# First block's attention: both key groups in one pass over the softmax, their matmuls on alternate halves of the array, compression in four column groups

## Chip, cores and metric

The kernel runs on one core of one Trainium2 chip. The metric is the device time of one execution in microseconds (us); the median of the runs shown is what is to be predicted.

## The reference

Two blocks of two layers each work on 256 tokens of width 1024, all in float32. Only the attention of the first block is touched by the change. Its branch A is compressed, selected and windowed attention, branch B a sliding window with sinks, branch C a latent attention:

```python
def nsa_attention(q, kc, vc, ks, vs, kw, vw, gate_logits, ...):
    G, R, dh = A_KV_GROUPS, A_HEADS // A_KV_GROUPS, HEAD_DIM      # 2, 4, 64
    k_cmp = compress_blocks(kc, tok, pos_k, w1_k, w2_k)           # gelu(flat @ w1) @ w2
    v_cmp = compress_blocks(vc, tok, pos_v, w1_v, w2_v)
    ...
    s = jnp.einsum('bqgrd,bngd->bgrqn', qc, k_cmp) * scale        # compressed
    ...
    s = jnp.einsum('bqgrd,bgqkd->bgrqk', qc, kb) * scale          # selected
    o_sel = jnp.einsum('bgrqk,bgqkd->bqgrd', p_sel, vb)
    s = jnp.einsum('bqgrd,bkgd->bgrqk', qc, kwc) * scale          # window
    o_win = jnp.einsum('bgrqk,bkgd->bqgrd', p_win, vwc)
    return gc[..., 0:1] * o_cmp + gc[..., 1:2] * o_sel + gc[..., 2:3] * o_win

merged = g_a * (o_a @ w_branch_a) + g_b * (o_b @ w_branch_b) + g_c * (o_c @ w_branch_c)
```

Branches A and B have 8 heads in 2 groups; the 4 heads of a group share keys and values of width 64.

## The kernel before

Linear layers split weights and activations into two float32r parts, `hi` and `lo` (`chunk` and `split`, lines 287 to 301): a chunk of 128x1024 weights is loaded by SP's queue into one of three `raw` buffers, ScalarE casts `hi` (L289) and VectorE subtracts `lo` (L290). Three matmuls (`mm3`, L305 to L307) replace one. A linear layer is a generator that yields after each chunk (12 matmuls of 512 columns where rows are tokens), so that it can be taken in steps. `first_layer` puts the gates of the branches and their output projections into the list `todo`, and `fill(n)` (L349) emits n chunks of it. Where a step stands in the program is then only a wish: a scheduler that knows the dependencies moves the instructions of each engine, and the order that results is fixed before the run.

`attention` (L638) has the stages B, C, compress (L809) and A, in this order. In B and A, a loop over two query tiles t of 128 tokens and over the two groups g calls `soft` for one group: for t = 0 one PSUM bank holds 4 heads of 128 keys, for t = 1 two banks hold 2 heads of 256 keys each. A bank starts with a mask (L537, bf16, an identity as weights) to which the scores are added (L685 in `heads`: the contraction is over the 64 rows of group g, rows 0 to 63 or 64 to 127). Then come the maximum (L542), the exponentials (L548), `fill(2)`, the reciprocal and the scaling (L557 to L562), the transposes into `ptp` (L567) and the copies to `PT` (L570, L572). `pv_group` (L575) multiplies with the values: 64 output columns, PSUM partitions 64g to 64g+63 of the bank `pob` or `poa`. A does this twice (kinds 0 and 1). C (L753, L759) works on four heads of one kind at a time; its value matmuls go to alternate halves of `poc`'s partitions for t = 0.

`compress` makes for keys and then for values a sum over 16 steps (L836): each has 32 weight columns (`kp`) and 256 columns of a raw float32 chunk, 4 steps to a chunk, all into partitions 0 to 31 of one bank. A GELU (L839), a transpose (L844) and a small matmul follow. The compressed scores are L777.

PSUM's 8 banks are shared out by `open_psum(3, 2, 3)`: 3 for linear layers, 2 for `po`, 3 short-lived ones.

A matmul of two float32 operands stands in the trace as two records, called passes here; a transpose, a bf16 or a float32r matmul as one.

## Time and profile before

| what | value |
|---|---|
| median of 3 runs | 3464.09 us (3457.46 to 3465.89) |
| the profiled execution | 3465.89 us, span 3465.9 us |
| TensorE (PE) busy | 3340.5 us, 96% of the span |
| VectorE (DVE), ScalarE (ACT) busy | 65%, 51% |
| mean granted TensorE clock | 0.985 of 2.4 GHz |

The profile shows one execution. Times of rows count from the start of the span. A matmul's duration reaches from its start to a modelled end, and the next starts before that end; how fast a row of matmuls runs is therefore read from start to start. Layer 0's attention lies at about 82 to 288 us, layer 1's at about 638 to 847 us.

### The profile page before, as it was taken

What the parts mean: (1) busy time and instruction counts of PE and PEld (TensorE: products, weight loads), DVE (VectorE), ACT (ScalarE), POOL (GpSimd) and SP (SyncE); (2) the same over time, 40 slices, a digit from 0 to 9 for tenths busy, and PEclk for the clock granted to TensorE, in tenths of its full rate; (3) what the DMA queues carried; (4) which work ended last, traced back from release to release, by engine and by line L of the source; (5) the groups of instructions that cost most, each with busy time, mean ns of one, the idle gap of its engine ahead of it and who ended that gap; (6) DMA issues with size and microseconds to landing.
All of it is one profiled execution on the core that took longest, in us unless ns stands there. A gap on an engine that the chain in (4) does not pass through costs nothing.

```text
span 3465.9 us, 53945 instructions
## 1 busy us (share of the span) xinstructions
PE 3340.5 (96%) x20862; PEld 2926.5 (84%) x20862; DVE 2255.5 (65%) x3879; ACT 1760.3 (51%) x3218; POOL 238.8 (7%) x159
## 2 busy tenths in 40 slices
PE   8999999999999999998999999998989899999999
PEld 6767998766898887898988999988879898899998
DVE  6646556646556875669965555557657996555555
ACT  4535445534445554444964444447444395444444
POOL 0000000000000000037000000000003700000000
PEclk9999999999999999998999999999999999999999
DMA  5344666443555444553255555555544415555555
GB/s 185 106 128 161 213 201 203 137 128 109 188 186 183 152 149 136 188 177 128 68 168 188 187 187 189 189 182 190 168 161 152 140 56 182 188 187 185 188 188 177
DMA packets 161105, 570.00 MB, mean 164 GB/s; under 512 B 18256, under 2 KB 23760, under 8 KB 159824
## 3 DMA queue, kind: packets, MB, share of 16 engines
q1 hardware_dynamic: 160848, 566.56, 49.7%
q8 instruction: 163, 2.67, 0.3%
q14 instruction: 94, 0.77, 0.1%
HBM read 557.05 MB, written 9.44 MB: 163 GB/s over the span
## 4 chain that ended last, share of the span: by engine, by line
PE 61%; DVE 10%; DMA 2%; ACT 2%; issue 1%; POOL 0%; DVEq 0%; POOLq 0%; ACTq 0%; SPq 0%
PE pacc L305 7%; PE pacc L307 7%; PE pacc L306 7%; PE aps L305 4%; PE aps L306 4%; PE aps L307 4%; PE ps L305 3%; PE ps L307 3%; PE ps L306 3%; PE gps L1681 3%; PE ps L1674 2%; PE fps L306 1%; PE fps L305 1%; PE fps L307 1%; DVE G L1767 1%; DVE lo L290 1%
## 5 line engine op out<-in xcount | busy, mean ns | idle before, releaser
L290 DVE TENSOR_TENSOR lo<-raw,hi 128x1024 fp32r<-128x1024 f32 (+3 forms) x906 | 1103.1, 1218 | 791.5 <-ACT hi L289 788.0
L289 ACT CAST hi<-raw 128x1024 fp32r<-128x1024 f32 (+1 forms) x978 | 1019.4, 1044 | 953.3 <-PE aps L306 182.4
L305 PE MATMUL pacc<-hi,pwh 128*128 128x512 f32 x1024 | 404.4, 395 | 0.1
L307 PE MATMUL pacc<-hi,pwl 128*128 128x512 f32 x1024 | 403.7, 394 | 0.0
L306 PE MATMUL pacc<-lo,pwh 128*128 128x512 f32 x1024 | 402.9, 393 | 0.0
L305 PE MATMUL aps<-xTh,hi 128*128 128x256 f32 x1296 | 365.1, 282 | 0.9 <-ACT G L1684 0.9
L306 PE MATMUL aps<-xTl,hi 128*128 128x256 f32 x1296 | 365.0, 282 | 0.0
L307 PE MATMUL aps<-xTh,lo 128*128 128x256 f32 x1296 | 363.6, 281 | 0.0
L305 PE MATMUL ps<-xTh,hi 128*128 128x256 f32 x960 | 278.4, 291 | 16.3 <-ACT hi L289 12.5
L307 PE MATMUL ps<-xTh,lo 128*128 128x256 f32 x960 | 277.8, 289 | 15.8 <-POOL lo L290 15.8
L289 ACT CAST pwh<-G 128x256 fp32r<-128x256 f32 x256 | 103.8, 406 | 342.7 <-DVE G L1689 213.9
L306 PE MATMUL ps<-xTl,hi 128*128 128x256 f32 x960 | 276.6, 288 | 1.2 <-DVE xTl L290 1.2
L305 PEld LDWEIGHTS aps<-xTh,hi 128*128 128x128 f32 x1296 | 243.8, 188 | 7.8 <-ACT G L1684 1.3
L306 PEld LDWEIGHTS aps<-xTl,hi 128*128 128x128 f32 x1296 | 243.7, 188 | 7.2
L307 PEld LDWEIGHTS aps<-xTh,lo 128*128 128x128 f32 x1296 | 243.8, 188 | 0.0
L307 PEld LDWEIGHTS pacc<-hi,pwl 128*128 128x128 f32 x1024 | 192.4, 188 | 45.9 <-DVE pwl L290 0.3
L305 PEld LDWEIGHTS pacc<-hi,pwh 128*128 128x128 f32 x1024 | 192.6, 188 | 39.0 <-ACT pwh L289 1.0
L306 PEld LDWEIGHTS pacc<-lo,pwh 128*128 128x128 f32 x1024 | 193.1, 189 | 37.9
L290 POOL TENSOR_TENSOR lo<-raw,hi 128x1024 fp32r<-128x1024 f32 x72 | 192.8, 2688 | 178.5 <-ACT hi L289 177.6
L305 PE MATMUL fps<-fTh,hi 128*128 128x256 f32 x704 | 199.6, 284 | 3.7 <-ACT fTh L289 3.6
L305 PEld LDWEIGHTS ps<-xTh,hi 128*128 128x128 f32 x960 | 187.6, 196 | 18.1 <-ACT hi L289 13.3
L307 PEld LDWEIGHTS ps<-xTh,lo 128*128 128x128 f32 x960 | 187.2, 195 | 17.5 <-POOL lo L290 17.2
(649 smaller groups left out, 7043.4 us busy)
## 6 DMA issues: line engine op xcount, KB each, us to landing
raw<-in_pu_dram SPq DMA_DIRECT2D x256, 512.0 KB, 3.3
raw<-in_pv_dram SPq DMA_DIRECT2D x256, 512.0 KB, 3.3
raw<-in_wbg_dram SPq DMA_DIRECT2D x48, 512.0 KB, 3.5
raw<-in_ffg_dram SPq DMA_DIRECT2D x44, 512.0 KB, 3.6
raw<-in_ffu_dram SPq DMA_DIRECT2D x44, 512.0 KB, 3.4
raw<-in_ffd_dram SPq DMA_DIRECT2D x44, 512.0 KB, 3.8
raw<-in_win_dram SPq DMA_DIRECT2D x36, 512.0 KB, 3.5
raw<-in_pwq_dram SPq DMA_DIRECT2D x32, 512.0 KB, 3.9
```

Source lines behind the costliest of these rows:

```text
L289: self.nc.scalar.copy(out=hi, in_=src)
L290: (eng or self.nc.vector).tensor_tensor(out=lo, in0=src, in1=hi.bitcast(F32), op=OP.subtract)
L305: mm(ps, lhsT=lh, rhs=rh, start=start, stop=False)
L306: mm(ps, lhsT=lh, rhs=rl, start=False, stop=False)
L307: mm(ps, lhsT=ll, rhs=rh, start=False, stop=stop)
L1674: nc.tensor.matmul(pi, lhsT=w[:, k * P:k * P + P], rhs=xT32[:, k], start=k == 0, stop=k == 7)
L1681: nc.tensor.matmul(ps[:, t * P:t * P + P], lhsT=A[:, t], rhs=B[:, t], start=True, stop=True)
L1767: nc.vector.tensor_tensor(out=cv[:, h], in0=vv[:, h, 0, :, None].to_broadcast([P, 16, 16]), in1=vv[:, h, 1, None, :].to_broadcast([P, 16, ...
```

## The change

- `soft` takes a list of score functions. For both groups it issues the two masks, then the scores head by head, group 0 and group 1 in turn; maxima, exponentials and sinks of both follow, then one `fill(4)`, then scaling, transposes and copies of group 0 and of group 1.
- `pv_groups` issues the value matmuls of both groups in turn for each key tile. In C the value matmuls go in turn to the two halves for t = 1 too.
- The compressed scores go in turn to two banks, one a group.
- In `compress` step j of a chunk goes to the PSUM partitions 32j to 32j+31. The four sums are copied to SBUF (`hq`, ScalarE) and added by a matmul with a 128x32 selection matrix `sel` into a new bank (`chs`).
- PSUM is shared out as 3, 1, 4.

```diff
-    def soft(self, pool, t, score_mm, mask, weight, sink=None):
+    def soft(self, pool, t, scores, mask, weights, sinks=None):
...
         for u in range(nk):
-            ps = self.bank("sc")
-            nc.tensor.matmul(ps.rearrange("p (a b) -> p a b", a=mask.shape[1]), lhsT=self.identb, rhs=mask, start=True, stop=False)
+            pss = [self.bank("sc") for _ in range(n)]
+            for ps in pss:
+                nc.tensor.matmul(ps.rearrange("p (a b) -> p a b", a=mask.shape[1]), lhsT=self.identb, rhs=mask, start=True, stop=False)
             for j in range(hb):
-                score_mm(ps[:, j * nk * P:(j + 1) * nk * P], u * hb + j, j == hb - 1)
...
+                for ps, score_mm in zip(pss, scores):
+                    score_mm(ps[:, j * nk * P:(j + 1) * nk * P], u * hb + j, j == hb - 1)
...
-        self.fill(2)
+        self.fill(2 * n)
...
-    def pv_group(self, ps, t, g, PT, v, start, stop):
+    def pv_groups(self, ps, t, PTs, v, start, stop):
...
         for kt in range(t + 1):
-            self.nc.tensor.matmul(ps[g * 64:g * 64 + 64, :], lhsT=v(kt), rhs=PT[:, kt].rearrange("p h q -> p (h q)"),
-                                  start=start and kt == 0, stop=stop and kt == t)
+            for g in range(2):
+                self.nc.tensor.matmul(ps[g * 64:g * 64 + 64, :], lhsT=v(kt, g), rhs=PTs[g][:, kt].rearrange("p h q -> p (h q)"),
+                                      start=start and kt == 0, stop=stop and kt == t)
...
-            self.open_psum(3, 2, 3)
+            self.open_psum(3, 1, 4)
...
-                    nc.tensor.matmul(hp[0:32, 0:256], lhsT=kp[:, jj].rearrange("p g n -> p (g n)"),
-                                     rhs=w[:, j * 256:j * 256 + 256], start=jj == 0, stop=jj == 15)
+                    nc.tensor.matmul(hp[j * 32:j * 32 + 32, 0:256], lhsT=kp[:, jj].rearrange("p g n -> p (g n)"),
+                                     rhs=w[:, j * 256:j * 256 + 256], start=c4 == 0, stop=c4 == 3, tile_position=(0, j * 32))
+
+            hq = ap.tile([P, 256], F32, tag="chq", name="chq", bufs=1)
+            nc.scalar.copy(out=hq, in_=hp[:, 0:256])
+            hs = self.bank("chs")
+            nc.tensor.matmul(hs[0:32, 0:256], lhsT=sel, rhs=hq, start=True, stop=True)
             hid = ap.tile([32, 256], F32, tag="chid", name="chid", bufs=2)
-            nc.scalar.activation(out=hid, in_=hp[0:32, 0:256], func=AF.Gelu_apprx_tanh)
+            nc.scalar.activation(out=hid, in_=hs[0:32, 0:256], func=AF.Gelu_apprx_tanh)
```

The order of SP's loads and of GpSimd's instructions is the same before and after, and so is TensorE's outside the two attentions but for a few rows. Three places on TensorE follow. In a row stand line, operation, output and inputs with buffer numbers, and the output's size; xN is a run of N.

Stage B of layer 0, between the first query tile and the second (`sc` scores, `mb` mask, `ptp` transposes, `pob` values, `ps` linear layer). Before:

```order
L567 MATMUL ptp_905<-cst_142,Pt_843 128x128 x4
L537 LDWEIGHTS identb_149
L537 MATMUL sc_918<-mb_156,identb_149 128x512
L685 MATMUL sc_918<-kT_247,qTb_246 128x256 x2
L578 MATMUL pob_772<-PT_904,vt_248 64x512
L537 LDWEIGHTS identb_149
L537 MATMUL sc_926<-mb_156,identb_149 128x512
L685 MATMUL sc_926<-kT_247,qTb_246 128x256 x2
L305 MATMUL ps_938<-hi_942,hTh_178 128x512
```

Now:

```order
L574 MATMUL ptp_904<-cst_142,Pt_774 128x128 x4
L539 LDWEIGHTS identb_149
L539 MATMUL sc_921<-mb_156,identb_149 128x512
L539 LDWEIGHTS identb_149
L539 MATMUL sc_922<-mb_156,identb_149 128x512
L588 MATMUL pob_772<-PT_892,vt_248 64x512
L588 MATMUL pob_772<-PT_903,vt_248 64x512
L695 MATMUL sc_921<-kT_247,qTb_246 128x256
L695 MATMUL sc_922<-kT_247,qTb_246 128x256
L695 MATMUL sc_921<-kT_247,qTb_246 128x256
L695 MATMUL sc_922<-kT_247,qTb_246 128x256
```

Scores of one group stood in a row and now alternate between the groups (`sc_921`, `sc_922`); the two value matmuls stand side by side.

Stage B of layer 0, after the second query tile's transposes. Before:

```order
L567 MATMUL ptp_981<-cst_142,Pt_915 128x128 x4
L567 MATMUL ptp_987<-cst_142,Pt_915 128x128 x4
L537 LDWEIGHTS identb_149
L537 MATMUL sc_998<-mb_156,identb_149 128x512
L685 MATMUL sc_998<-kT_247,qTb_246 128x256 x2
L578 MATMUL pob_914<-PT_980,vt_248 64x512 x2
```

Now:

```order
L574 MATMUL ptp_1059<-cst_142,Pt_916 128x128 x4
L574 MATMUL ptp_1065<-cst_142,Pt_916 128x128 x4
L588 MATMUL pob_914<-PT_1041,vt_248 64x512
L588 MATMUL pob_914<-PT_1058,vt_248 64x512
L588 MATMUL pob_914<-PT_1041,vt_248 64x512
L588 MATMUL pob_914<-PT_1058,vt_248 64x512
L389 MATMUL trp_1091<-cst_142,cxn_1083 128x128 x2
```

Mask and scores of the other group stood between transposes and values; now the values follow the transposes at once.

From compress to A in layer 0 (`chp` compression, `chs` the added sum, `scm` compressed scores). Before:

```order
L836 MATMUL chp<-raw,kp 32x256 x16
L844 MATMUL chT<-cst,chid 128x32 x2
L853 MATMUL cko<-chTk,cw2d 128x32 x2
L821 MATMUL cps<-cst,vt 64x64 x8
L836 MATMUL chp<-raw,kp 32x256 x16
L305 MATMUL ps<-hi,oTh 128x512 x2
L844 MATMUL chT<-cst,chid 128x32 x2
L306 MATMUL ps<-lo,oTh 128x512
```

Now:

```order
L847 MATMUL chp<-raw,kp 32x256 x16
L853 MATMUL chs<-chq,csel 32x256
L860 MATMUL chT<-cst,chid 128x32 x2
L869 MATMUL cko<-chTk,cw2d 128x32 x2
L832 MATMUL cps<-cst,vt 64x64 x8
L847 MATMUL chp<-raw,kp 32x256 x16
L853 MATMUL chs<-chq,csel 32x256
L860 MATMUL chT<-cst,chid 128x32 x2
```

Each half has one matmul more, and no row of a linear layer stands in the stage any longer.

## Rows read from the trace of the kernel before

**Rows 1.** The page: busy time and its share of the span, by engine.

```profile
PE 3340.5 (96%) x20862; PEld 2926.5 (84%) x20862; DVE 2255.5 (65%) x3879; ACT 1760.3 (51%) x3218; POOL 238.8 (7%) x159
```

**Rows 2.** By stretch: us, busy PE, PEld, DVE, ACT, POOL, granted clock, DMA share, GB/s.

```profile
82.10:124.50 42.40, 41.87 (x181) 28.39 (x181) 26.22 (x50) 22.72 (x61) 0.00 (x0) 1.00 0.37 119
...
175.50:200.30 24.80, 20.80 (x111) 11.19 (x111) 5.14 (x16) 4.75 (x6) 0.53 (x1) 0.92 0.58 188
200.30:288.00 87.70, 87.70 (x374) 58.79 (x375) 54.77 (x91) 38.42 (x95) 0.31 (x1) 0.98 0.34 108
...
757.00:847.50 90.50, 90.50 (x375) 61.04 (x375) 54.84 (x91) 38.35 (x95) 0.31 (x1) 0.95 0.33 104
```

**Rows 3.** Timeline of PE in stage B: start, us, engine, line, what, count.

```profile
90.58 0.38 PE L537 MATMUL sc<-mb,identb 128*128 128x512 bf16 x1
90.89 1.16 PE L685 MATMUL sc<-kT,qTb 64*128 64x128 f32 x8
91.98 0.50 PE L306 MATMUL ps<-lo,hTh 128*128 128x512 f32 x1
92.40 1.07 PE L578 MATMUL pob<-PT,vt 128*64 128x512 f32 x2
93.41 0.50 PE L307 MATMUL ps<-hi,hTl 128*128 128x512 f32 x1
93.75 0.39 PE L305 MATMUL ps<-hi,hTh 128*128 128x512 f32 x1
93.98 0.39 PE L306 MATMUL ps<-lo,hTh 128*128 128x512 f32 x1
```

**Rows 4.** Tiles sc, pob, poa, scm: passes of the run, ns min/median/max, forms.

```profile
L685 PE MATMUL sc<-kT,qTa x128: 272/376/579, 203.7 to 833.4; 64*128 64x128 f32 x64, 64*128 64x256 f32 x64
...
L578 PE MATMUL pob<-PT,vt x24: 592/592/644, 92.4 to 678.8; 128*64 128x512 f32 x24
...
L578 PE MATMUL poa<-PT,vt x48: 592/592/643, 213.4 to 845.7; 128*64 128x512 f32 x48
...
L777 PE MATMUL scm<-kcT,qTa x64: 259/259/373, 198.7 to 798.2; 64*128 64x16 f32 x64
```

**Rows 5.** Timeline of PE in stage A: runs on one half alone.

```profile
235.21 1.06 PE L777 MATMUL scm<-kcT,qTa 64*128 64x16 f32 x8
...
249.51 1.93 PE L578 MATMUL poa<-PT,vt 128*64 128x512 f32 x4
```

**Rows 6.** Timeline of PE: runs where two halves meet (C, compress, second block).

```profile
139.74 0.66 PE L759 MATMUL poc<-PT,vc 128*64 128x128 f32 x8
...
198.90 0.84 PE L777 MATMUL scm<-kcT,qTa 64*128 64x16 f32 x10
...
2441.80 0.83 PE L1552 MATMUL hsp<-hv,hf 64*128 64x128 f32 x9
```

**Rows 7.** Timeline of all engines in compress, layer 0.

```profile
175.56 7.09 PE L836 MATMUL chp<-raw,kp 128*32 128x256 f32 x32 [0.61 <-PE cps L821]
177.47 0.33 SPq L295 DMA_DIRECT2D raw<-in_cw1k_dram  x1
...
185.83 8.75 PE L836 MATMUL chp<-raw,kp 128*32 128x256 f32 x32 [0.85 <-DVE kp L829]
...
196.59 0.72 PE L305 MATMUL ps<-hi,oTh 128*128 128x512 f32 x2 [2.01 <-ACT hi L289]
```

**Rows 8.** Tile raw, 172 to 200 us: load issue to landing.

```profile
DMA to landing us min/median/max: 3.2/4.1/4.7
```

**Rows 9.** Groups of DVE, 80 to 300 us: busy, mean ns, idle before.

```profile
L290 DVE TENSOR_TENSOR lo<-raw,hi 128x1024 fp32r<-128x1024 f32 x40 | 48.9, 1221 | 22.0 <-ACT hi L289 21.8
L572 DVE COPY PT<-ptp 128x512 f32<-128x512 f32 x16 | 11.0, 690 | 11.7 <-PE ptp L567 11.7
L542 DVE TENSOR_REDUCE nm<-sc 128x2 f32<-128x512 f32 x16 | 10.9, 688 | 10.1 <-PE sc L685 9.0 <-PE sc L753 1.1
L562 DVE TENSOR_TENSOR Pt<-Pt,rc 128x1024 f32<-128x1024 f32 x8 | 9.8, 1225 | 0.3
```

More of the change, by code (lines that the diff above doesn't have):

```diff
@@ L531, in soft @@
         hb = 4 // nk
-        Pt = pool.tile([P, 4, 2 * P], F32, tag="Pt", name="Pt", bufs=2)[:, :, :nk * P]
-        nm = pool.tile([P, 4], F32, tag="nm", name="nm", bufs=4)
-        sm = pool.tile([P, 4], F32, tag="sm", name="sm", bufs=4)
+        n = len(scores)
+        Pts = [pool.tile([P, 4, 2 * P], F32, tag="Pt", name="Pt", bufs=2)[:, :, :nk * P] for _ in range(n)]
+        nms = [pool.tile([P, 4], F32, tag="nm", name="nm", bufs=4) for _ in range(n)]
+        sms = [pool.tile([P, 4], F32, tag="sm", name="sm", bufs=4) for _ in range(n)]
@@ L550, in soft @@
-        if sink is not None:
-            es = pool.tile([P, 4], F32, tag="es", name="es", bufs=2)
-            nc.vector.tensor_tensor(out=es, in0=sink, in1=nm, op=OP.add)
-            nc.scalar.activation(out=es, in_=es, func=AF.Exp)
-            nc.vector.tensor_tensor(out=sm, in0=sm, in1=es, op=OP.add)
-        self.fill(2)
-        rc = pool.tile([P, 4], F32, tag="rc", name="rc", bufs=4)
-        nc.vector.reciprocal(rc, sm)
-        if weight is not None:
-            nc.vector.tensor_tensor(out=rc, in0=rc, in1=weight, op=OP.mult)
-        else:
-            nc.vector.tensor_scalar(rc, rc, 0.5, None, op0=OP.mult)
@@ L562, in soft @@
-        nc.vector.tensor_tensor(out=Pt, in0=Pt, in1=rc[:, :, None].to_broadcast([P, 4, nk * P]), op=OP.mult)
-        PT = pool.tile([P, 2, 4, P], F32, tag="PT", name="PT", bufs=2)
-        for kt in range(nk):
-            ps = self.bank("ptp")
-            for h in range(4):
-                nc.tensor.transpose(ps[:, h * P:h * P + P], Pt[:, h, kt * P:kt * P + P], self.ident)
-            dst = PT[:, kt].rearrange("p h q -> p (h q)")
-            if kt:
-                nc.scalar.copy(out=dst, in_=ps)
-            else:
-                nc.vector.tensor_copy(dst, ps)
@@ L573, in soft @@
-        return PT
-    def pv_group(self, ps, t, g, PT, v, start, stop):
+                for ps, score_mm in zip(pss, scores):
+                    score_mm(ps[:, j * nk * P:(j + 1) * nk * P], u * hb + j, j == hb - 1)
+            for i in range(n):
+                pv = pss[i].rearrange("p (j k) -> p j k", j=hb)
+                hs = slice(u * hb, u * hb + hb)
+                nc.vector.tensor_reduce(out=nms[i][:, hs], in_=pv, axis=AX, op=OP.max, negate=True)
+                if sinks is not None:
+                    nc.vector.scalar_tensor_tensor(out=nms[i][:, hs], in0=sinks[i][:, hs], scalar=-1.0, in1=nms[i][:, hs],
+                                                   op0=OP.mult, op1=OP.min)
+                for j in range(hb):
+                    h = u * hb + j
+                    nc.scalar.activation(out=Pts[i][:, h], in_=pv[:, j], func=AF.Exp, bias=nms[i][:, h:h + 1],
+                                         accum_out=sms[i][:, h:h + 1])
@@ new lines, in soft @@
+        if sinks is not None:
+            for sink, nm, sm in zip(sinks, nms, sms):
+                es = pool.tile([P, 4], F32, tag="es", name="es", bufs=2)
+                nc.vector.tensor_tensor(out=es, in0=sink, in1=nm, op=OP.add)
+                nc.scalar.activation(out=es, in_=es, func=AF.Exp)
+                nc.vector.tensor_tensor(out=sm, in0=sm, in1=es, op=OP.add)
+        self.fill(2 * n)
+        PTs = []
+        for i in range(n):
+            rc = pool.tile([P, 4], F32, tag="rc", name="rc", bufs=4)
+            nc.vector.reciprocal(rc, sms[i])
+            if weights is not None:
+                nc.vector.tensor_tensor(out=rc, in0=rc, in1=weights[i], op=OP.mult)
+            else:
+                nc.vector.tensor_scalar(rc, rc, 0.5, None, op0=OP.mult)
+            nc.vector.tensor_tensor(out=Pts[i], in0=Pts[i], in1=rc[:, :, None].to_broadcast([P, 4, nk * P]), op=OP.mult)
+            PT = pool.tile([P, 2, 4, P], F32, tag="PT", name="PT", bufs=2)
+            for kt in range(nk):
+                ps = self.bank("ptp")
+                for h in range(4):
+                    nc.tensor.transpose(ps[:, h * P:h * P + P], Pts[i][:, h, kt * P:kt * P + P], self.ident)
+                dst = PT[:, kt].rearrange("p h q -> p (h q)")
+                if kt:
+                    nc.scalar.copy(out=dst, in_=ps)
+                else:
+                    nc.vector.tensor_copy(dst, ps)
+            PTs.append(PT)
@@ L813, in compress @@
         nc.gpsimd.memset(V2, 0.0)
+        sel = ap.tile([P, 32], F32, name="csel")
+        nc.vector.tensor_reduce(out=sel, in_=self.ident.rearrange("p (j n) -> p n j", j=4), axis=AX, op=OP.add)
         for s in "kv":
```

44 lines of the change are left out of this document (17 added, 27 removed).

## The prediction

> **What bounds the kernel now.** I read the page first: TensorE is busy for 96% of the span, VectorE for 65%, ScalarE for 51% [rows 1]. An average hides stages, so the table by stretch came next. In stage B of layer 0 TensorE is busy for 41.87 of 42.40 us, in stage A for all of 87.70; VectorE has 26.22 and 54.77 us there [rows 2]. The reader is to see that `fill` covers the softmax fully: time taken off TensorE in B and A comes off the run, as long as VectorE does not become the next bound. Compress is different: busy for 20.80 of 24.80 us at a mean granted clock of 0.92, with little else to do [rows 2]. Last came the timeline, read from start to start, for what a pass and a change of the array's shape cost.
>
> **Prices.** A lone 64-row pass of 128 columns or fewer takes (1.06 - 0.26) / 7 = 0.114 us [rows 4, 5]. A pass of 256 columns takes (7.09 - 0.38) / 31 = 0.216 us in compress's run of 32 [rows 7]; 0.38 is how long one such pass lasts, the median of the `sc` row, whose longer half are the 256-column passes [rows 4]. A value pass of 512 columns takes (1.93 - 0.59) / 3 = 0.45 us with the run's slow first one, 0.43 without [rows 4, 5]. A linear matmul starts every 0.23 us (93.75 to 93.98) [rows 3].
>
> Now the change of shape. From 90.58 to 93.75 stand a mask, 8 score passes, a linear matmul, 2 value passes and another linear one: 3.17 us [rows 3]. At the prices above they need 0.23 + 8 x 0.113 + 0.23 + 2 x 0.43 + 0.23 = 2.45. The other 0.72 us fall to four changes between whole array, row halves and column halves: **0.18 us each**.
>
> **Do two halves overlap?** This kernel already has places where they meet. In C eight passes of 128 columns on alternate column halves last 0.66 us [rows 6]; the last starts 0.66 - 0.27 = 0.39 after the first [a pass of 128 columns lasts 0.27 at least, rows 4], where one half alone would need 7 x 0.114 = 0.80. For row halves, ten passes of the compressed scores where the groups meet start every (0.84 - 0.26) / 9 = 0.064 us, nine of the second block's 64-row passes every (0.83 - 0.27) / 8 = 0.07, against 0.114 alone [rows 5, 6]. So both kinds run side by side in float32, and I take the longer of two equal runs: half.
>
> **The sum for one layer.** A has 32 score passes of 128 and 32 of 256 columns a layer (rows 4, two layers), B half as many; the scores stand alternately now.
> - Scores: of 48 passes of 128 columns 24 go, 24 x 0.113 = 2.7 us; of 48 of 256 columns 24 go, 24 x 0.216 = 5.2. Together 7.9.
> - Values: 72 passes in both layers [rows 4], 36 in one; 18 x 0.43 = 7.7.
> - Compressed scores: 64 passes in both [rows 4], 32 in one; 16 x 0.114 = 1.8.
> - Changes of shape outside compress, counted in the two whole orders for one layer: 75 before, 44 now. 31 x 0.18 = 5.6.
> - C's values alternate already at t = 0; the second tile gains a few tenths, taken as nothing. Masks, transposes, exponentials, copies, fill chunks and loads keep their number. A's first pair changes shape once more between its two masks; that is in the 44.
> - Bound from the other side: new waits. In four of a layer's six pairs the values follow the transposes at once, where a mask and scores stood between. They then wait for a copy of 0.69 us [rows 9]: 4 x 0.7 = 2.8 lost. One `po` bank in place of two costs nothing: four fill chunks (4 x 12 x 0.23 = 11 us) stand between the last read of one and the first write of the next.
>
> **Compress.** The keys' 32 passes took 7.09 us, and the fourth chunk's load, which waits for the first chunk's buffer, went out at 177.47, 1.91 after the start [rows 7]. In four column groups a chunk of 8 passes needs 2 x 0.216 = 0.43, so this load goes out 1.3 earlier, about 176.2, lands 3.2 later [rows 8] at 179.4, and the keys end near 179.8 in place of 182.65. From there to the values' start it was 185.83 - 182.65 = 3.2 us; the added copy, the matmul of two passes and their handovers make it about 4.4 (0.4 + 0.6 + 0.2, an estimate from the 256-column pass and a shape change). The values start at 184.2; their fourth load goes out 0.5 later, lands 4.1 later at 188.8, and they end at 189.2, where it was 185.83 + 8.75 = 194.58. The second added chain gives back 1.2: **4.2 us gained**, bound by loads instead of matmuls. Ends: all the matmul time saved, three quarters of 64 x 0.216, 10.4; or nothing, with both chains paid, -2.4. No row shows four column groups at once, but two at once would move the end by less than 1 us, since the loads decide.
>
> Sum: 7.9 + 7.7 + 1.8 + 5.6 + 4.2 - 2.8 = 24.4 a layer, 48.8 for two. The profiled execution took 3465.9, 1.8 above the median; 3465.9 - 48.8 = 3417.1, and against the median **3415**.
>
> **Rivals.**
> *VectorE takes over (0.15).* B's 26.22 us of VectorE now stand in about 35 us, A's 54.77 in about 72: 75%. A second-tile pair has four maxima (2.8 us), small steps (about 1.8), two scalings (2.4) and up to four `lo` (4.9) in one queue, 11.9 us, and some 2 us of exponentials inside the chain, against 11.1 us of fill [rows 9]. If all of it comes before the last transposes, 2.9 us a pair are open, some 0.7 for a first-tile pair: 3 x 3.6 = 10.8 a layer, leaving 13.6, 27 in all: 3437. Against: in ScalarE's order three chunks' `hi` stand ahead of A's first exponentials, and in VectorE's only one `lo` between B's two scalings. The Trainium skill, "TensorEngine Tiling (Array Packing)", section "PSUM Bottleneck", states this rule: packing speeds up TensorE but not the emptying of PSUM, which may become the bound. No row here shows it happening yet.
>
> *A slot lost in each run (0.07).* Every float32 matmul is two passes of one half. If starts keep program order strictly, the first group's second pass must go before the second group's first, and each run takes one slot more: three runs of 0.113, six of 0.216 and six of 0.43 a layer, 4.2 us, leaving 40: 3424. Against: four matmuls on alternate halves would need five slots, a last start at 4 x 0.114 = 0.46; it was 0.39 [rows 6]. The Trainium skill, "TensorE: Matmul & The Clock Gate", section "Part 3: Packing small matmuls — row/col tiling", says just this of order, and also that a weight load passes running matmuls only where the row group differs. By that, column pairs would also wait for each load of 64 columns, by its price for a load, columns over 1.2 GHz, 53 ns each: an estimate of 36 x 0.053 = 1.9 us a layer more, 3428 with the lost slots. The trace's 0.66 us for eight passes on column halves disagrees.
>
> *It does not do what it says (0.08).* The long passes do not overlap, say because two streams of 256 or 512 columns cannot be read at once; the rows that overlap have 16 to 128. Only the shapes and compress remain: 5.6 + 4.2 - 2.8 = 7.0, 14 in all: 3450.
>
> *Slower, by the clock (0.03).* In compress TensorE stood at its lower level of 1.2 GHz for 2 x 0.08 x 24.8 = 4 us, and in the A after it for 3.5 us in layer 0 and 9 in layer 1 [rows 2]. Now compress has a quarter of its matmul time and longer idle stretches. If the clock then stayed low through both A stages (2 x 72 us, less the 12.5 they lose part of already), the run takes 143 - 6 = 137 us more for that and 49 less for the change: 3552. It decides where 98 us more are spent at the lower level. Against: in B, with many small passes, the clock was 1.00, and the longest stretch at the lower level is those 9 us [rows 2].
>
> **How the numbers follow.** The forecast has 0.67, with its own range 3397 (no new waits, 10.4 in compress) to 3428 (compress at -2.4). With the first two rivals that makes 0.89, so the range is 3397 to 3440. About 0.3% (10 us) is what a measurement of this kernel can tell from no change: forecast, both first rivals and half of the third are faster, 0.93; the other half the same, 0.04; slower 0.03.
>
> **What would show it.** Right: `sc` and value passes of both groups start in twos, some 10 ns apart, at the lone pass's pace; B shorter by some 6 us, A by 15; TensorE still busy throughout in both; the loads' landing, not matmuls, ending the waits in compress. Wrong: `ptp` waiting for `Pt` (VectorE), `pob` and `poa` for `PT` by more than 0.7 each, a granted clock in A under 0.9, or single starts at 0.216 and 0.43.

## The result

The changed kernel takes 3419.33 us (median of four runs, 3416.98 to 3424.47), the kernel before 3464.80 beside it. The ratio is **0.9874**, 95% interval 0.9861 to 0.9887. The prediction was 3415 (3397 to 3440). The profiled execution of the changed kernel has a span of 3419.2 us; all that follows is read from it and from the profiled executions of the experiments.

The page, busy time by engine, beside [rows 1]:

```profile
PE 3283.9 (96%) x20870; PEld 2901.5 (85%) x20870; DVE 2251.0 (66%) x3881; ACT 1759.0 (51%) x3222; POOL 240.1 (7%) x159
```

TensorE lost 56.6 us of busy time and the span 46.7, with the share at 96% as before. Nearly all of the difference is compress's, where TensorE lost 17.3 busy us and the stage only 7.9 (next two tables).

By stretch, first the kernel before, cut at marks that every run has: stage B of layer 0 (first mask to last `pob` pass), compress (first `cps` to first `scm` pass) and stage A (first `scm` to last value pass) of layer 0, then the last two of layer 1. Every mark is the start of its pass. The columns are those of [rows 2].

```profile
82.12:122.20 40.08, 39.95 (x174) 27.33 (x174) 25.08 (x47) 21.04 (x55) 0.00 (x0) 1.00 0.36 116
172.94:198.65 25.71, 21.16 (x128) 11.41 (x127) 5.04 (x16) 4.90 (x7) 0.53 (x1) 0.93 0.50 164
198.65:287.15 88.50, 88.50 (x389) 60.14 (x388) 55.74 (x95) 39.24 (x95) 0.31 (x1) 0.98 0.34 109
729.50:755.28 25.78, 21.16 (x129) 11.50 (x128) 4.75 (x16) 5.26 (x8) 0.53 (x1) 0.93 0.50 163
755.28:846.72 91.44, 91.44 (x389) 62.50 (x388) 56.22 (x95) 38.97 (x95) 0.31 (x1) 0.94 0.33 105
```

The same five stretches of the changed kernel:

```profile
80.70:114.11 33.41, 33.41 (x170) 24.39 (x170) 23.04 (x46) 20.23 (x54) 0.00 (x0) 1.00 0.46 139
165.11:186.01 20.90, 12.22 (x130) 6.99 (x129) 3.19 (x14) 4.78 (x8) 0.53 (x1) 0.78 0.55 194
186.01:263.31 77.30, 77.02 (x387) 55.92 (x387) 56.76 (x96) 39.84 (x96) 0.31 (x1) 0.95 0.39 126
698.03:720.71 22.68, 12.78 (x129) 7.08 (x128) 3.19 (x14) 5.14 (x9) 0.53 (x1) 0.75 0.56 186
720.71:798.55 77.84, 77.56 (x388) 56.30 (x387) 56.76 (x96) 39.18 (x96) 0.31 (x1) 0.94 0.39 123
```

B of layer 0 is 6.7 us shorter (part of it, 0.9 us, are four transposes that now stand behind B), A 11.2 and 13.6, compress 4.8 and 3.1. In B and A TensorE is still busy throughout. In compress it is not: 12.22 of 20.90 us, where it had 21.16 of 25.71, and the granted clock fell from 0.93 to 0.78 and 0.75. From the first mask of B to the last value pass of A the two layers together take 368.1 us where they took 413.1. This sum, called **both attentions** below, is what the experiments are compared by; all else in the program kept its order but for a few rows.

TensorE's timeline in stage B of layer 0, beside [rows 3] and [rows 5], with one row of its weight loads (PEld) and the first score passes of A (188.37); the count is in passes:

```profile
80.70 0.60 PE L539 MATMUL sc<-mb,identb 128*128 128x512 bf16 x2
81.23 1.16 PE L695 MATMUL sc<-kT,qTb 64*128 64x128 f32 x16
82.33 0.50 PE L305 MATMUL ps<-hi,hTh 128*128 128x512 f32 x1
...
94.98 1.65 PE L588 MATMUL pob<-PT,vt 128*64 128x512 f32 x4
95.55 0.19 PEld L588 LDWEIGHTS pob<-PT,vt 128*64 128x64 f32 x2 [0.39 <-DVE PT L579]
96.56 1.14 PE L695 MATMUL sc<-kT,qTb 64*128 64x256 f32 x8
...
112.36 2.35 PE L588 MATMUL pob<-PT,vt 128*64 128x512 f32 x8
...
188.37 0.80 PE L695 MATMUL sc<-kT,qTa 64*128 64x128 f32 x2
```

Sixteen score passes now last 1.16 us, as long as eight did in [rows 3]: they start in twos, 6 to 7 ns apart, a pair every 0.112 us. One exception stands in each layer: in A's first pair a mask stands behind one group's first two passes (188.37), so four of its sixteen run alone. The values pair only in part. Four passes last 1.65 us, eight 2.35; full pairs would need one and three steps of 0.43 plus the last pass's 0.59, so 1.02 and 1.88. The second group's passes start 0.58 us after the first's in the one, 0.42 in the other: they wait for that group's `PT` copy (95.55).

Compress of layer 0, all engines, beside [rows 7]:

```profile
167.46 1.50 PE L847 MATMUL chp<-raw,kp 128*32 128x256 f32 x24 [0.56 <-DVE kp L840]
...
168.16 0.33 SPq L295 DMA_DIRECT2D raw<-in_cw1k_dram  x1
...
171.54 0.64 PE L847 MATMUL chp<-raw,kp 128*32 128x256 f32 x8 [2.57 <-DMA raw<-in_cw1k_dram]
172.24 0.37 ACT L851 COPY chq<-chp 128x256 f32<-128x256 f32 x1 [5.04 <-PE chp L847]
...
172.63 1.28 ACT L855 ACT_TABLE_LOAD   x1
...
172.67 0.62 PE L853 MATMUL chs<-chq,csel 128*32 128x256 f32 x2 [0.49 <-ACT chq L851]
173.93 0.37 ACT L855 ACTIVATE chid<-chs 32x256 f32<-32x256 f32 x1
...
177.89 2.69 PE L847 MATMUL chp<-raw,kp 128*32 128x256 f32 x24 [0.69 <-issue]
...
182.24 0.64 PE L847 MATMUL chp<-raw,kp 128*32 128x256 f32 x8 [1.65 <-DMA raw<-in_cw1v_dram]
```

Four column groups do run at once: 24 passes in 1.50 us, starts some 7 ns apart within a four. The landing of the fourth chunk now ends the wait, 2.57 us for the keys and 1.65 for the values. And one thing was not foreseen: ScalarE's table load (1.28 us), which before lay under the keys' matmuls (175.26 in that trace), now stands behind the new copy, so that `chid` starts 0.64 us after `chs` has ended (172.67 + 0.62 to 173.93).

### The profile page after: what moved, and what is told of

The parts are those of the page before. It is cut to its first block, busy times and chain, and to the rows that moved or that the text cites. A ratio compares the mean times of both kernels' runs of the same rounds, so it can differ in the third digit from the quotient of the medians.

```text
span 3419.2 us, 53950 instructions
## 1 busy us (share of the span) xinstructions
PE 3283.9 (96%) x20870; PEld 2901.5 (85%) x20870; DVE 2251.0 (66%) x3881; ACT 1759.0 (51%) x3222; POOL 240.1 (7%) x159
## 4 chain that ended last, share of the span: by engine, by line
PE 62%; DVE 11%; ACT 2%; DMA 1%; issue 1%; POOL 0%; DVEq 0%; POOLq 0%; ACTq 0%; SPq 0%
PE pacc L305 7%; PE pacc L307 7%; PE pacc L306 7%; PE aps L305 5%; PE aps L306 4%; PE aps L307 4%; PE ps L307 3%; PE ps L305 3%; PE ps L306 3%; PE gps L1697 3%; PE ps L1690 2%; PE fps L305 1%; PE fps L306 1%; PE fps L307 1%; DVE G L1783 1%
## 5 line engine op out<-in xcount | busy, mean ns | idle before, releaser
L307 PEld LDWEIGHTS ps<-xTh,lo 128*128 128x128 f32 x960 | 186.3, 194 | 16.5 <-POOL lo L290 16.3
```

The costliest lines, as they stand in the source:

```text
L307: mm(ps, lhsT=ll, rhs=rh, start=False, stop=stop)
```

## The experiments

The ratio is that to the kernel before on the same chip, with its 95% interval; the last column are the microseconds at the lower of TensorE's two clock levels (1.2 GHz of 2.4) in compress and A of both layers, out of the granted clock of these stretches (0.95 over 77.30 us is 2 x 0.05 x 77.3 = 8).

| kernel | median us | ratio | both attentions | compress | A | lower level |
|---|---|---|---|---|---|---|
| before | 3464.8 | 1 | 413.1 | 25.7, 25.8 | 88.5, 91.4 | 20.5 |
| changed | 3419.3 | 0.9874 (0.9861 to 0.9887) | 368.1 | 20.9, 22.7 | 77.3, 77.8 | 37.6 |
| scores by group | 3430.7 | 0.9895 (0.9879 to 0.9912) | 375.5 | 22.6, 22.5 | 79.6, 80.8 | 51.2 |
| values by group | 3422.1 | 0.9869 (0.9853 to 0.9886) | 368.5 | 21.9, 21.9 | 77.2, 77.9 | 41.0 |
| both by group | 3428.6 | 0.9892 (0.9875 to 0.9908) | 373.8 | 20.6, 21.9 | 81.1, 80.0 | 41.0 |
| masks between | 3446.3 | 0.9953 (0.9938 to 0.9969) | 389.6 | 22.6, 22.4 | 85.1, 84.0 | 47.8 |
| values later | 3415.1 | 0.9864 (0.9849 to 0.9879) | 366.6 | 22.7, 21.3 | 77.2, 77.4 | 44.4 |
| compress undone | 3430.9 | 0.9904 (0.9888 to 0.9921) | 375.5 | 24.7, 24.0 | 78.7, 78.7 | 23.9 |
| compress alone | 3463.6 | 0.9995 (0.9986 to 1.0005) | 412.9 | 22.3, 23.3 | 93.1, 92.6 | 54.6 |
| copy on VectorE | 3431.4 | 0.9910 (0.9895 to 0.9925) | 375.2 | 24.0, 23.7 | 78.7, 79.5 | 51.2 |
| work moved in | 3429.9 | 0.9909 (0.9896 to 0.9923) | 374.7 | 24.6, 25.4 | 79.7, 78.9 | 41.0 |
| TensorE kept busy | 3430.1 | 0.9902 (0.9885 to 0.9919) | 376.5 | 25.9, 27.5 | 76.8, 76.8 | 17.1 |
| two chains | 3413.0 | 0.9853 (0.9837 to 0.9868) | 356.2 | 17.6, 16.0 | 77.8, 75.3 | 20.5 |
| two chains, values later | 3411.5 | 0.9848 (0.9835 to 0.9861) | 356.8 | 17.3, 17.1 | 77.8, 76.5 | 30.7 |

The program outside the attentions differs by up to 11 us between these profiled executions (3045.8 us in "values later", 3056.4 in "scores by group" and "masks between"), though no edit touches it, so a few microseconds of median alone carry no verdict; the stretches carry more. They vary too: compress is the same program in the six rows from "changed" to "values later", and both layers of it together take 42.6 to 45.2 us, at granted clocks of 0.64 to 0.79; the A behind it has 7.7 to 12.0 us a layer at the lower level.

**Does the alternate order do it?**

```diff
-            for j in range(hb):
-                for ps, score_mm in zip(pss, scores):
+            for ps, score_mm in zip(pss, scores):
+                for j in range(hb):
...
-            for r in range(4):
-                for g, ps in enumerate(pss):
+            for g, ps in enumerate(pss):
+                for r in range(4):
```

> The changed kernel with the scores, and the compressed scores, of a merged pair issued group after group instead of in alternation; the masks, the values and the compression stay as changed. Theory (only matmuls of different row halves that follow each other directly run at once): the whole terms of scores and compressed scores go, 2 x (7.9 + 1.8) = 19.4 us, so about 3439 us. Rival (the engine runs the second group's first passes while about three passes of the first are left, as the halves that meet in [rows 6] suggest): of the eight passes of a group of query tile 0 five are lost at 0.11 us, of query tile 1 one of four at 0.216 us, some 4.1 us a layer, so about 3427 us. Telling rows: the score passes in the trace, start to start, in the stretch of the first attention.

Both attentions are 7.4 us longer: near the rival's 8.2, far from the theory's 19.4. The score rows have 4.9 of it (from start to start over B and A of both layers, `sc` 33.7 to 36.9 and `scm` 6.5 to 8.1); some 1.5 are in compress, which this run leaves alone, and the rest in A's other passes, with 2.7 us more at the lower level. Two runs of TensorE's timeline in B of this kernel:

```profile
81.03 1.71 PE L695 MATMUL sc<-kT,qTb 64*128 64x128 f32 x16
...
96.91 1.14 PE L695 MATMUL sc<-kT,qTb 64*128 64x256 f32 x8
```

Group after group, sixteen passes take 1.71 us where alternation needs 1.16 and one behind the other would need 15 x 0.112 = 1.68 and the last pass's 0.27. In the trace's starts the fifth pass of the first group is at 81.579 and the first of the second group at 81.585, three places ahead of its turn. Runs of four passes (256 columns) therefore overlap whole: 1.14 us, the same as alternating. So TensorE took up a pass of the other row half while three of the first were still to start.

The same for the values:

```diff
-        for kt in range(t + 1):
-            for g in range(2):
+        for g in range(2):
+            for kt in range(t + 1):
```

> The changed kernel with the value matmuls of query tile 1 issued group after group (both key tiles of group 0, then both of group 1); at query tile 0, which has one key tile, nothing changes. Theory (only directly following column halves run at once): of two runs of four passes of 0.43 us one is laid behind the other, less the present delay of 0.3 to 0.4 us of the second group, some 1.4 us in each of three places of a layer, 8 us in all, so about 3427 us. Rival (passes of the other half are taken up while about three of the first are left, or the second group's values are late anyway because of their copy): at most 0.2 us a place, so 3419 to 3421 us.

368.5 us against 368.1: no difference, as the rival says. Runs of values are four passes long at most. Which of the rival's two reasons holds, the passes taken up early or the late copy, this run does not tell. And both edits together:

> The changed kernel with scores, compressed scores and values all issued group after group inside a merged pair: what is left of the change is that both groups' softmax goes side by side (fewer changes of shape) and the four column groups of the compression. Theory (only direct alternation overlaps): the sum of the two runs before, +19.4 and +8 us, about 3447 us, and against the kernel before some 18 us are left (changes of shape 2 x 5.6 and compression 2 x 4.8, less the new waits). Rival (the engine takes up the other half some three passes early): about 3428 us.

373.8 us, again the rival, with the same 36.9 and 8.1 us in the score rows. Most of the gain in B and A comes from the two groups standing next to each other; the order inside the pair is worth some 5 us in both layers, all of it where a group has eight passes.

**What does a mask between the groups cost?**

```diff
-            for ps in pss:
+            for ps, score_mm in zip(pss, scores):
                 nc.tensor.matmul(ps.rearrange("p (a b) -> p a b", a=mask.shape[1]), lhsT=self.identb, rhs=mask, start=True, stop=False)
-            for j in range(hb):
-                for ps, score_mm in zip(pss, scores):
+                for j in range(hb):
```

> The changed kernel with each group's mask matmul directly ahead of that group's scores, so that a pair reads mask, scores, mask, scores; all else as changed. Theory (it is that the groups stand next to each other that counts, since the engine passes by up to three waiting passes of the other half, and a whole-array matmul between them ends that): all overlap of the scores goes, 24 passes of 128 and 24 of 256 columns a layer, 7.9 us, and two changes of shape more in each of nine runs, 18 x 0.18 = 3.2 us: 11 us a layer, 22 us in all, some 15 us more than the run with the scores group after group; both attentions together 390 us where the changed kernel has 368. Rival (a change of shape costs little in itself, what I priced at 0.18 us is the end of a run that nothing overlaps): 16 us, both attentions 384 us.

389.6 us, where the theory said 390 and the rival 384; 3446 where the two said 3441 and 3435. TensorE's timeline in B of this kernel:

```profile
79.73 0.39 PE L539 MATMUL sc<-mb,identb 128*128 128x512 bf16 x1
80.05 1.16 PE L695 MATMUL sc<-kT,qTb 64*128 64x128 f32 x8
81.14 0.39 PE L539 MATMUL sc<-mb,identb 128*128 128x512 bf16 x1
81.46 1.16 PE L695 MATMUL sc<-kT,qTb 64*128 64x128 f32 x8
82.54 0.51 PE L305 MATMUL ps<-hi,hTh 128*128 128x512 f32 x1
```

Mask and scores of both groups take 2.81 us (79.73 to 82.54), in the changed kernel 1.63 (80.70 to 82.33). A mask of the whole array ends the overlap. From one mask to the next are 1.41 us; the mask's 0.23 and 8 x 0.113 leave 0.28 for two changes of shape, 0.14 each, where 0.18 was predicted. Of the 21.5 us over the changed kernel 1.3 are in compress, unedited here, and some 2 are the clock's, an estimate at the 0.43 us worked out below, for 4.4 us more at the lower level in A. Without these the total lies between the two forecasts, and it is the rows that decide for the theory: sixteen passes with no overlap, and a price for each change of shape.

**The late copies.**

```diff
-        self.fill(2 * n)
+        self.fill(2 * n - (n > 1))
...
             PTs.append(PT)
-        return PTs
+        self.fill(n > 1); return PTs
```

> The changed kernel with one of the four chunks of linear work moved from ahead of a pair's transposes to behind them, ahead of its value matmuls, so that the copies out of PSUM have 2.8 us of cover. Theory (the second group's value matmuls start 0.58, 0.42, 0.13, 0.58, 0.42 and 0.30 us after the first's in a layer because its copy comes later; with the copies covered they start some 10 ns apart): 2.4 us a layer less, 4.8 us in all, about 3415 us. Rival (with three chunks of cover instead of four the scaled weights are not there in time, and the transposes wait): the gain is eaten or turned, 3419 to 3428 us, and the trace shows ptp waiting for Pt.

3415.1, the theory's number, but not for its reason alone. TensorE's timeline in B of this kernel:

```profile
93.64 1.08 PE L588 MATMUL pob<-PT,vt 128*64 128x512 f32 x4
...
110.95 1.94 PE L588 MATMUL pob<-PT,vt 128*64 128x512 f32 x8
```

With the copies covered the value passes pair fully: 1.08 and 1.94 us, not 1.65 and 2.35. B is 0.9 and 0.8 us shorter, A 0.1 and 0.4 with a linear pass more. No transpose waits for `Pt`. Both attentions keep 1.5 us of it, where 4.8 were expected; in the profiled execution 5.3 us more are gone outside the attentions, where nothing was edited. So the theory's mechanism came, and that its number came too is luck. The interval of the ratio overlaps the changed kernel's: that this edit alone makes the kernel faster is not shown.

**What is the compression worth?** First undone in the changed kernel:

```diff
-                    nc.tensor.matmul(hp[j * 32:j * 32 + 32, 0:256], lhsT=kp[:, jj].rearrange("p g n -> p (g n)"),
-                                     rhs=w[:, j * 256:j * 256 + 256], start=c4 == 0, stop=c4 == 3, tile_position=(0, j * 32))
+                    nc.tensor.matmul(hp[0:32, 0:256], lhsT=kp[:, jj].rearrange("p g n -> p (g n)"),
+                                     rhs=w[:, j * 256:j * 256 + 256], start=jj == 0, stop=jj == 15)
...
-            hq = ap.tile([P, 256], F32, tag="chq", name="chq", bufs=1)
-            nc.scalar.copy(out=hq, in_=hp[:, 0:256])
-            hs = self.bank("chs")
-            nc.tensor.matmul(hs[0:32, 0:256], lhsT=sel, rhs=hq, start=True, stop=True)
...
-            nc.scalar.activation(out=hid, in_=hs[0:32, 0:256], func=AF.Gelu_apprx_tanh)
+            nc.scalar.activation(out=hid, in_=hp[0:32, 0:256], func=AF.Gelu_apprx_tanh)
```

> The changed kernel with the compression as before the change: all sixteen matmuls of a kind into one column group, no copy of the four partial sums and no matmul that adds them; the merged pairs stay. Theory (the gain between the first matmul of the compression and the first compressed score, 25.7 to 20.9 us in the two traces, belongs to the four column groups alone): +4.8 us a layer, about 3429 us. Rival (part of it is paid back in the third attention, whose clock is at the lower level for some 10 us in the changed kernel and for 3.4 us before): the compression is 4.8 us longer and the third attention 2 to 3 us shorter in each layer, so about 3423 to 3425 us, and the granted clock over the first 10 us of the third attention is near that of before.

Then alone: the kernel before with the changed `compress` (the same lines the other way round) and nothing else.

> The kernel before with the changed compression alone (four column groups, the copy and the adding matmul); its attention goes group by group as before. Theory (the compression's gain stands by itself, as the run with the compression undone says: 3.5 us of a layer's compression plus a little more): 7 to 11 us faster than the kernel before, about 3455 us, and the merged pairs are worth the other 35. Rival (with four column groups TensorE is idle for longer and its clock is lower for longer, which the third attention pays for): the compression itself is 4 us a layer shorter, the third attention up to 3 us longer, so 2 to 4 us faster only, about 3461 us.

Undone it costs 7.4 us in both attentions, 5.1 of them in compress itself. The rival's A, 2 to 3 us shorter, did not come: A was 1.4 and 0.9 us longer. Compress and A of layer 0 with the compression undone:

```profile
164.76:189.45 24.69, 20.98 (x128) 11.19 (x128) 4.33 (x15) 4.77 (x7) 0.52 (x1) 0.93 0.54 166
189.45:268.17 78.72, 78.43 (x386) 56.75 (x384) 55.97 (x95) 39.05 (x96) 0.31 (x1) 0.93 0.38 123
```

Alone it brings nothing that can be measured: 0.9995, at best 0.9986 by the interval, which is 5 us. The stretches of that run, compress and A of each layer, as above:

```profile
171.33:193.63 22.30, 14.01 (x129) 7.45 (x128) 3.19 (x14) 5.13 (x9) 0.52 (x1) 0.65 0.53 187
193.63:286.75 93.12, 93.12 (x392) 63.98 (x391) 58.15 (x96) 39.74 (x96) 0.31 (x1) 0.94 0.31 104
727.86:751.16 23.30, 14.04 (x130) 7.45 (x129) 3.19 (x14) 5.14 (x9) 0.52 (x1) 0.64 0.53 181
751.16:843.73 92.57, 92.57 (x391) 63.54 (x391) 58.17 (x96) 39.59 (x96) 0.31 (x1) 0.94 0.31 104
```

Compress is 3.4 and 2.5 us shorter than before, A 4.6 and 1.1 longer. Three linear passes a layer moved from compress into A (x392 for x389): 1.4 us. The clock accounts for most of the rest: it was at the lower level for 54.6 us where before had 20.5; in A 22.5 against 13.7. What a microsecond there costs, the two layers of the kernel before say: A took 91.45 - 88.50 = 2.95 us more for 6.83 more at the lower level (10.24 against 3.41), 0.43 for one. By that estimate 8.9 x 0.43 = 3.8; with the 1.4 that makes 5.2 of the 5.7 us.

**The chain inside compress.** The copy of the partial sums by VectorE:

```diff
-            nc.scalar.copy(out=hq, in_=hp[:, 0:256])
+            nc.vector.tensor_copy(hq, hp[:, 0:256])
```

> The changed kernel with the copy of the four partial sums in the compression done by VectorE instead of ScalarE. Theory (ScalarE loads its table for the activation only after that copy, 1.28 us on the way from the keys' end to the values' start; without the copy it loads it earlier, as in the kernel before): the chain of the keys shrinks from 5.7 to about 4.4 us in each layer, 2.6 us in all, about 3417 us. Rival (the values then wait as long for their fourth load): nothing, 3419 us.

Slower, which neither said. The table load did go ahead of the copy, but the keys' chain did not shrink (170.94 to 176.55, 5.6 us): `chs` took 1.06 us at the lower clock level where it had 0.62. The first row here is TensorE's; the other two stand in ScalarE's timeline at the values' end:

```profile
171.49 1.06 PE L853 MATMUL chs<-chq,csel 128*32 128x256 f32 x2 [0.55 <-DVE chq L851]
...
184.08 1.04 ACT L289 CAST hi<-raw 128x1024 fp32r<-128x1024 f32 x1 [11.12 <-DMA raw<-in_wbb_dram]
185.03 0.37 ACT L855 ACTIVATE chid<-chs 32x256 f32<-32x256 f32 x1
```

Without the copy on ScalarE, the order written for that engine puts a linear chunk's cast ahead of `chid`. The cast waits for its load, and `chid` waits behind it, about 1.5 us after `chs` was done. In the changed kernel `chid` (184.22) stands ahead of that cast (184.76): the copy had been holding its place in the queue. This wait is some 3 us, over both layers, of the 7.1 in both attentions; A's clock, at the lower level for 4.9 us more, is some 2 by the price above.

Then linear work put into the gaps:

```diff
-        self.fill(2 * n)
+        self.fill(2 * n if t or n == 1 else 2 * n - 1)
...
+            self.fill(1 if s == "k" else 2)
             hq = ap.tile([P, 256], F32, tag="chq", name="chq", bufs=1)
```

> The changed kernel with three chunks of linear work a layer moved from the pairs of query tile 0 into the compression, one ahead of the keys' copy of the partial sums and two ahead of the values'. Theory (TensorE has some 8 us a layer with nothing to do there, and its clock is at the lower level for 37.6 us around the two third attentions where it was 20.5 before; work in these gaps fills them and keeps the clock up): 3 to 6 us a layer, 3407 to 3413 us, with fewer microseconds at the lower level. Rival (the chunks' loads stand in the same queue and the same three buffers as the compression's own, and delay it; or the pairs with three chunks wait for their weights): 3419 us or more.

The rival. Of the 36 linear passes written into compress the scheduler left 12 there; the others ended up in A. TensorE's timeline in compress of layer 0:

```profile
179.62 1.50 PE L847 MATMUL chp<-raw,kp 128*32 128x256 f32 x24
183.62 0.64 PE L847 MATMUL chp<-raw,kp 128*32 128x256 f32 x8 [2.51 <-DMA raw<-in_cw1v_dram]
```

Compress has these 12 passes more, 2.8 us, and is 3.7 and 2.7 us longer: nothing of them was hidden. In TensorE's order they stand ahead of the values' `chp`, which now starts 16.5 us after the first `cps` pass, not 12.8, and still waits 2.5 us for its fourth chunk. What linear work inside these waits would bring, this run does not say.

Then matmuls that compute nothing, so that TensorE is busy while it waits (one of five places shown):

```diff
+            idle = lambda n, ps=ps: [nc.tensor.matmul(ps[:, 256:384], lhsT=self.ident, rhs=self.ident, start=True, stop=True) for _ in range(n)]
...
             for c4 in range(4):
+                if c4 == 3:
+                    idle(22 if s == "k" else 6)
```

> The changed kernel with 51 matmuls of 128 columns a layer more in the compression (identity times identity, into columns of the cps bank that nobody reads), placed where TensorE waits: for the fourth chunks, for the copy, for the activation. They add some 5.6 us of work into some 8.7 us of waiting and nothing that anyone waits for, save a few tenths where a wait is shorter. Theory (the clock's lower level around the third attention, 37.6 us in the changed kernel, comes from TensorE's waiting in the compression, and is what ate the compression's gain in the run that had it alone): the microseconds at the lower level fall to 10 or less, the third attention is some 3.5 us a layer shorter (0.43 us for each us at the lower level, from the two layers before: 91.45 - 88.50 over 10.24 - 3.41), 3411 to 3413 us. Rival (the clock falls whatever TensorE does there, as it did for 10.24 us in both third attentions of the run with the compression undone, where TensorE waits less): lower-level time as in the changed kernel, 3419 to 3422 us.

I had mis-sized it: a 128-column float32 matmul is two passes of 0.112 us (in the trace's starts, 172.541 to 177.231 for 42 steps), so 51 of them were 11.4 us of work, not 5.6, and compress grew by 5. As a measurement of the clock it stands all the same. The longest run of them, then compress and A of each layer:

```profile
172.33 5.18 PE L834 MATMUL cps<-cst 128*128 128x128 f32 x44
...
166.46:192.40 25.94, 22.89 (x231) 17.44 (x230) 3.19 (x14) 4.67 (x8) 0.52 (x1) 1.00 0.45 155
192.40:269.16 76.76, 76.46 (x388) 55.27 (x387) 56.78 (x96) 39.77 (x96) 0.31 (x1) 0.96 0.40 127
707.52:735.06 27.54, 24.48 (x232) 18.66 (x231) 3.19 (x14) 4.79 (x9) 0.52 (x1) 0.94 0.42 151
735.06:811.83 76.77, 76.47 (x389) 55.26 (x387) 56.79 (x96) 39.58 (x96) 0.31 (x1) 0.96 0.38 125
```

With TensorE at work in compress the granted clock there is 1.00 and 0.94, not 0.78 and 0.75, and A is 0.5 and 1.1 us shorter than in the changed kernel, with the same work. So with TensorE's waits filled the clock hardly falls inside compress. That this decides the clock in A is not shown: each A still has 6.8 us at the lower level, not far under the 7.7 to 12.0 of the runs that leave compress as changed, and the run with the compression undone has 10.2 there after a compress that was busy for 20.98 of 24.69 us. What decides the lower level in A stays open.

**A version that beats both.** The values' `cps`, `kp` and first three chunks go ahead of the keys' tail:

```diff
-        for s in "kv":
...
+        kk, hk = front("k")
+        chunks("k", kk, hk, 0, 4)
+        kv, hv = front("v")
+        chunks("v", kv, hv, 0, 3)
+        tail("k", hk)
+        chunks("v", kv, hv, 3, 4)
+        tail("v", hv)
```

> The changed kernel with the compression's two kinds overlapped: the values' first part (cps, kp and the first three chunks of chp) is issued ahead of the keys' tail (copy, adding matmul, activation, transposes, cko), the values' fourth chunk behind it; kp has two buffers. Theory (the compression is a chain of handovers and landings, of which the 5.7 us from the keys' end to the values' start are pure waiting; the values' fourth load goes out as soon as their first chunk is done): 4 to 5 us a layer less, about 3410 us. Rival (the loads come one behind the other whatever the order, and the values' loads land no earlier): 0 to 2 us a layer, 3415 to 3419 us.

3413.0, and 356.2 us in both attentions, 11.9 less than the changed kernel, 10.0 of them in compress: the theory, with 4 to 5 us a layer. Compress of layer 0:

```profile
168.48 1.50 PE L849 MATMUL chp<-raw,kp 128*32 128x256 f32 x24 [0.56 <-DVE kp L840]
...
172.51 0.64 PE L849 MATMUL chp<-raw,kp 128*32 128x256 f32 x8 [1.91 <-DMA raw<-in_cw1k_dram]
173.21 0.37 ACT L854 COPY chq<-chp 128x256 f32<-128x256 f32 x1 [4.99 <-PE chp L849]
...
173.89 0.64 PE L849 MATMUL chp<-raw,kp 128*32 128x256 f32 x8 [0.74 <-DMA raw<-in_cw1v_dram]
...
179.22 1.08 PE L849 MATMUL chp<-raw,kp 128*32 128x256 f32 x8
```

The values' first chunk runs 0.7 us after the keys' last one (173.89), under the keys' copy and table load, and their last chunk at 179.22, 13.1 us after the first `cps` pass (166.13), where it was 17.1 (182.24 less 165.11). Compress takes 17.6 and 16.0 us, its clock is 0.87 and 0.89, and layer 1's A has only 3.4 us at the lower level.

> The run with the compression's two kinds overlapped, and one chunk of linear work of a pair moved from ahead of the transposes to ahead of the value matmuls, as in the run with the values later. Theory (the two gains lie in different stages and add): some 4 us less than the run with the two kinds overlapped alone, about 3406 us. Rival (what the one gains, the clock or the loads take back in the other): no less than the better of the two, 3410 to 3415 us.

3411.5 and 356.8 us: not to be told from the run before. The rival holds; B is shorter by 0.9 and 0.8 us, A of layer 1 longer with 6.7 us at the lower level instead of 3.4. Both versions are faster than the kernel before; against the changed kernel the first one's interval overlaps at the edge, and the second one's ends where the changed kernel's begins (0.9861), so the 6 to 8 us between the medians are likely and the 12 us of the stretches are the firmer sign.

## Why the prediction was right, and where it was not

The forecast case came: pairs, full cover, gains in all three stages, 3419 for 3415. B was to be some 6 us shorter and was 6.7 and 6.1; A was to be 15 shorter and was 11.2 and 13.6. The terms, for two layers, against TensorE's time from each pass's start to the next start, summed by tile over B and A (the values' row has the few passes of the compressed values too):

| term | predicted | before to changed |
|---|---|---|
| scores, with their masks | 15.8 | 51.7 to 33.7: 18.0 |
| compressed scores | 3.6 | 7.6 to 6.5: 1.1 |
| values, new waits | 15.4 - 5.6 | 36.7 to 22.9: 13.8; transposes 15.7 to 16.7: -1.0 |
| changes of shape | 11.2 | in the linear passes 144.9 to 140.9: 4.0; the rest is in the rows above |
| compress | 8.4 | 51.5 to 43.6: 7.9 |

*Scores: right*, nearly to the pass: 0.112 us a pair for 0.113, and all pairs found but for A's first, where four of sixteen passes are alone. The reason given was half of it. "Stand alternately now" is worth some 5 us; standing side by side is what counts, and the run with masks between lost all of it.

*Values and new waits: mis-sized.* The waits were priced at four copies a layer, 5.6 us in two layers. They show as second-group starts 0.13 to 0.58 us late, 2.4 us a layer at the value passes; covering the copies took 3.4 us off the value passes in two layers (22.9 to 19.5) and 1.5 off both attentions.

*Changes of shape: mis-sized the other way.* The price was a little high: 0.14 where the run with masks between shows it alone, which for 31 fewer changes a layer is 8.7 us in two layers, not 11.2. What is left for it after the passes is an estimate: 2.2 us in the scores' row (18.0 less 15.8), 3.5 in the linear one (4.0 less two passes fewer) and, with the copies covered, 1.8 in the values' (36.7 to 19.5, less 15.4), 7.5 in all. The two errors, waits priced too high and changes of shape too high, cancel in part.

*Compressed scores: mis-sized, 3.6 for 1.1.* The sixteen passes of the first query tile in the changed kernel, then with TensorE kept busy:

```profile
186.01 1.89 PE L786 MATMUL scm<-kcT,qTa 64*128 64x16 f32 x16
192.40 1.17 PE L786 MATMUL scm<-kcT,qTa 64*128 64x16 f32 x16
```

The prediction priced them at the full clock; those of the first query tile ran at the lower level. With TensorE kept busy the row is 5.0 instead of 6.5, 2.7 under before. The rest of the error is in the sum: it halved all 64 passes, though the ten of [rows 6] show that in the first query tile the two groups met, and overlapped in part, before the change.

*Compress: right in its sum, by luck in its parts.* Keys' end 7.1 us after the first `cps` pass, 2.6 earlier than before (predicted 2.85). The chain from there to the values 5.7 us, not 4.4: the table load and the lower clock. The values' fourth load went out 1.1 us after their start, not 0.5, and landed 3.2 later, not 4.1, which cancels. The chain's loss was made up at the end, where the copy keeps `chid` ahead of the casts. And the step "4.2 us gained" silently took A's time as independent: alone, in the kernel before, the same edit gave nothing. Why it costs 7.4 us to undo beside merged pairs but brings nothing without them is not settled: the lower-level time in A differs (22.5 us alone, 17.2 here), but it is 17.0 to 21.6 in the runs that leave compress as changed, and 3.4 and 10.2 us in the two layers of the kernel before, with the same work ahead of both.

*The rivals.* VectorE did not take over: 56.76 of 77.30 us, 73%, and TensorE waits 0.3 us in all of A. The long passes do overlap: eight of 256 columns last 1.14 us (96.56), and with the copies covered four value passes last 1.08. No slot was lost: pairs start together and end together. On this the Trainium skill, "TensorE: Matmul & The Clock Gate", section "Part 3: Packing small matmuls — row/col tiling", says that matmuls keep strict program order at start and end; in the run with the scores by group a pass of the other half started ahead of three that stood before it (81.585), and the measurement decides. Of the slower rival the first step came, at a hundredth of its price: compress did idle more and the clock did fall, 37.6 us at the lower level for 20.5, but it came back within 8 to 9 us of A. The 3.5 us more in A cost 1.5, an estimate at 0.43.

## What to carry to other kernels

Bring work for different halves of the array next to each other first, with no whole-array matmul between. Whether it then alternates made no difference here with four passes of one half in a row, and some 5 us in all with eight. When matmuls in a chain of handovers get shorter, ask what the engine does in the time set free: here the shorter compression alone took 5.9 us off its own stage, and the stage behind it grew by 5.7, by estimate mostly at the lower clock. Laying a second chain under the wait was worth more (11.9 us in both attentions) than speeding up the first (7.4). Look at each in-order queue before removing a small instruction from it: it may hold the place of what follows.

## What the runs showed of the hardware

- TensorE started a row half's pass ahead of three waiting passes of the other half (81.585 beside 81.579), and of none across a whole-array mask (80.05 to 82.54 in the run with masks between).
- Four column groups of 32 run together: 24 passes of 256 columns in 1.50 us, where one group took 7.09 for 32 [rows 7].
- A whole-array to row-half change of shape cost 0.14 us, an estimate from the 1.41 us between two masks.
- The granted clock in compress of layer 0 was 0.93 at 21.16 busy us of 25.71, 0.78 at 12.22 of 20.90 and 1.00 at 22.89 of 25.94, but 0.65 at 14.01 of 22.30 in the run with the compression alone. Whatever it was, 3.4 to 12.0 us of the A behind it, in all runs and both layers, were at the lower level.
